# Who issues the stores of the normalised tiles: the load queue's engine or ScalarE

## The chip, the core and the metric

The kernel runs on one core of a Trainium2 chip. A core has five engines with instruction queues of their own: TensorE (PE, matrix products, with its weight loads shown as PEld), VectorE (DVE), ScalarE (ACT), GpSimd (POOL) and SyncE (SP). Here SP computes nothing: it only issues DMA transfers. Sixteen DMA engines do the moving. The metric is the device time of one execution in microseconds (us), the median of several runs.

## The reference

One inference step of a two-layer decoder on 1024 prompt positions and 8 decode positions, model width 2048, all in float32. Layer 0 is a pooling mixer, layer 1 a sliding-window attention; shared keys and values are projected between them.

```python
z = x @ w_in                       # 2048 -> 4096
u, gate = z[..., :2048], z[..., 2048:]
d = pool(u) - u                    # trailing windows 2/4/8/16 on four channel groups
y = (group_linear(d) * scale * silu(gate)) @ w_out
h = layer_norm(ALPHA * x + y)      # layer 0, the normalised tiles "h"
...
k, v = h @ w_kv                    # shared keys and values
q, gate = h @ w_in_b               # 2048 -> 4096
o = window_attention(q, k, v, sinks) * silu(gate)
y = layer_norm(ALPHA * h + o @ w_out_b)
```

Only the two `layer_norm` lines and the way in which their results leave the core are touched here.

## The kernel before

**Layout and phases.** Activations lie transposed: 128 channels on the partitions, positions along the free axis. The positions are cut into chunk 0 (512 positions) and chunk 1 (520: 512 prompt, 8 decode). The work runs as phases (`PHASES`, line 50): `ai` (input projection, pooling and gate of layer 0), `ao` (its output projection), `bi` (query and gate projections with attention), `bo` (output projection of layer 1), each for chunk 0 and chunk 1. The products are float32 made of rounded float32r parts: every weight tile and every activation tile is split into a high part (an ACT cast, line 506 or 839) and a low part (a DVE subtraction, line 521 or 848), and three matmuls per tile (lines 685 to 687, or 713 to 715) add high by high, high by low and low by high.

**Products.** Most phases use seven products in place of eight (Strassen's scheme): `seven` (line 597) runs products in the order 0, 2, 1, 5, 3, 4, 6 into three PSUM banks; each product is 24 matmuls. Between products small ACT and DVE instructions move bank contents: after product 0 ACT copies a bank negated into another (`p0`, line 624), after product 2 into SBUF (`p2`, line 630), after 1 (`p1`, line 633), after 5 (`p5`, line 639), after 3 (`p3`, line 645, with a DVE subtraction, line 646), after 6 (`p6`, line 658). They are written into the queues when the next product begins, so each has about one product's time before TensorE needs the bank again. Phase `bi` of chunk 0 begins with two plain parts (`unit`, line 699) of 24 wider matmuls per weight tile.

**The weight stream.** `begin` (line 533) keeps a stream of weight tiles of 512 KB going: loads (line 288, on SP) run up to seven tiles ahead of the products, casts four, low parts three. In the plain parts these are five, four and three. All buffers come from one pool of 54 slots in SBUF (`Mem`, line 140), so a load waits until the slot's last user is done.

**Layer norm.** `ln_gen` (line 985) is a generator that runs beside a later product phase, one step per product. It finishes the sums, makes the mean and the reciprocal deviation, then goes over eight tiles of 128 partitions by two by 512 (or 520) values: load the tile (line 998, SP), subtract the mean (line 1072, DVE; chunk 0 alone), multiply (line 1075, DVE), scale and shift by two ACT activations (line 1064), and store (line 1065). It is used three times: the tiles of `h` of chunk 0 during `ao` of chunk 1, of `h` of chunk 1 at the start of `bi` of chunk 0, and the output tiles `y0` of chunk 0 during `bo` of chunk 1, the last phase. `h` is read back later by line 829 (tiles for products) and line 1329 (residuals); of `h`, DVE also makes sums and differences of the same tiles in SBUF (lines 896 to 899), which POOL stores (line 900). The output of chunk 1 has code of its own at the end (`phase_end`, lines 1416 and on, with its stores at line 1503).

**Order.** The order of PE, DVE and ACT instructions is that of the source (`in_order`, line 86). The order on SP and POOL is set by the tile framework's scheduler. Each DMA counts up a counter when it has landed; the DMAs that SP and ACT issue take eight counters in turn (`DMAHW0` to `DMAHW7`), and a DMA is issued only when the one that used its counter before has landed.

Of the kernel before, what the change touches and what calls it, by code (L numbers as in the profile page):

```python
# [191 lines left out]
class Kern:  # L192
# [792 lines left out]
    def ln_gen(self, c, pre, acc, gc, bc, out, td):  # L985


        nc = self.nc
        T = CHUNKS[c][1]
        pre = dict(enumerate(pre))  # L990
        away = lambda p: self.act["p", c][:, 2 * p : 2 * p + 2, :]
        L = self.mem.full(2 * T)
        mu, rr = L.a[:, :T], L.a[:, T : 2 * T]

        def load(p):
            if p < 8 and p not in pre:
                pre[p] = self.mem.full(2 * T)
                nc.sync.dma_start(self.pair_view(pre[p], T), away(p))

        b2 = lambda x: x[:, None, :].to_broadcast([P, 2, T])  # L1000
        flat = lambda s: s.a[:, : 2 * T]
        a2 = self.pair_view(acc, T)
        load(0)
        mean, var = {}, {}
        put = lambda s, ps: nc.scalar.copy(mu[:, s], ps)
        if c == 0:
            s2 = self.pair_view(self.l_sq[0], T)
            steps = (
                self.j_steps(T, a2[:, 0], a2[:, 1], mean, acc), self.j_steps(T, s2[:, 0], s2[:, 1], var, self.l_sq[0])
            )  # L1010
            for k in range(3):
                for st in steps:
                    st[k]()
                yield
        else:
            yield
        yield from self.quiet()
        load(1)
        if c == 0:
            self.j_sum(T, mean, put)  # L1020
        else:
            self.j_sum32(T, [a2[:, 0], a2[:, 1]], put)
            acc.free()
        yield
        w = self.mem.full(2 * T)
        q, v = w.a[:, :T], w.a[:, T : 2 * T]
        if c == 0:
            nc.vector.tensor_mul(q, mu, mu)
        else:
            sq, sqs = self.mem.full(2 * T), {}  # L1030
            for p in range(10):
                load(p + 2)
                if p < 8:
                    t = self.pair_view(pre[p], T)
                    nc.vector.tensor_sub(t, t, b2(mu))
                if 1 <= p <= 8:
                    sqs[p - 1] = sq if p == 1 else self.mem.full(2 * T)
                    nc.scalar.activation(flat(sqs[p - 1]), flat(pre[p - 1]), AF.Square)
                yield
                if p > 2:  # L1040
                    nc.vector.tensor_add(flat(sq), flat(sq), flat(sqs[p - 2]))
                    sqs[p - 2].free()
                yield
            s2 = self.pair_view(sq, T)
            for go in self.j_steps(T, s2[:, 0], s2[:, 1], var, sq):
                go()
                yield
        yield from self.quiet()
        self.j_sum(
            T, var,  # L1050
            lambda s, ps: nc.vector.scalar_tensor_tensor(v[:, s], ps, EPS, q[:, s], op0=ALU.add, op1=ALU.subtract)
            if c == 0 else nc.vector.tensor_scalar(v[:, s], ps, EPS, None, op0=ALU.add),
        )
        yield
        self.rstd(v, rr, q)
        w.free()
        yield

        def affine(p):
            t = self.pair_view(pre[p], T)  # L1060
            for j in range(2):
                m = 2 * p + j
                g, b = (self.prm[:, i + m : i + m + 1] for i in (gc, bc))
                nc.scalar.activation(t[:, j], t[:, j], AF.Identity, bias=b, scale=g)
            nc.sync.dma_start(out[:, 2 * p : 2 * p + 2, :], t)

        for p in range(10):
            load(p + 2)
            if p < 8:
                t = self.pair_view(pre[p], T)  # L1070
                if c == 0:
                    nc.vector.tensor_sub(t, t, b2(mu))
                    if td is None:
                        yield
                nc.vector.tensor_mul(t, t, b2(rr))
            if 1 <= p <= 8:
                affine(p - 1)
                if td is None:
                    pre[p - 1].free(True)
            if td is not None:  # L1080
                yield
            if p >= 2 and td is not None:
                t = self.pair_view(pre[p - 2], T)
                self.t_ops(t[:, 0], t[:, 1], td, p - 2, T // 2)
                pre[p - 2].free(True)
            yield
        L.free()
# [1423 lines left out]
```

## Time and profile before

| | |
|---|---|
| three runs | 2311.78, 2307.44, 2310.27 us, median 2310.27 |
| the profiled execution | 2308.12 us, of which the span from first to last instruction is 2306.3 |
| mean granted TensorE clock over the span | 0.998 |
| DVE, ACT, POOL busy | 83%, 60%, 9% of the span |
| bytes moved by DMA | 654 MB, 284 GB/s on average |
| transfers issued by SP at line 1065 | 24 (16 of `h`, 8 of `out_y`) |

The profile is of one execution. A row of the timeline gives start, duration, engine, line, operation and tiles by name; equal neighbours are merged (`x2`), and their time then covers the wait between them. A row of the waits names who waited, who released it, the total in us, how often, and the longest. In the chain of waits each row is a piece of the path that ended last, with its start and length. `SPq` is SP's queue.

### The profile page before, as it was taken

To read this page: it belongs to the slowest core of one execution; us is meant where nothing else is said; L and a number is where in the kernel's file an instruction comes from. 1 tells how busy PE (TensorE), PEld (TensorE's weight loads), DVE (VectorE), ACT (ScalarE), POOL (GpSimd) and SP (SyncE) were. 2 spreads that over 40 slices of the span, in tenths; PEclk is the share of its full clock that TensorE was granted. 3 is DMA by queue.
4 is the path that set the end of the run, shared out by engine and by line. 5 is a ranking of instruction groups with operands and counts; after the bars stand their busy time and mean duration, and the time that the engine had idled before them with its cause. 6 is when DMAs were issued, how large, how long until landed. Compare 5 with 4: busy or idle time off the path is not lost.

```text
span 2306.3 us, 50594 instructions
## 1 busy us (share of the span) xinstructions
PE 2283.7 (99%) x20353; PEld 2213.7 (96%) x20353; DVE 1908.0 (83%) x2429; ACT 1387.0 (60%) x2551; POOL 218.8 (9%) x399
## 2 busy tenths in 40 slices
PE   9999999999999999999999999999999999999998
PEld 8999999999999999999879999999999999999998
DVE  8888889877878888998868888899876777878987
ACT  5544446544546546555566666785766768657655
POOL 0111110011010010000111111101100010000001
PEclk9999999999999999999999999999999999999999
DMA  7868679988889999999676666777787878799884
GB/s 259 282 248 308 234 254 325 320 301 295 304 310 313 344 352 374 328 381 364 210 265 235 229 238 231 276 273 265 254 269 230 272 266 295 242 325 335 285 304 149
DMA packets 256956, 654.07 MB, mean 284 GB/s; under 512 B 27824, under 2 KB 116944, under 8 KB 256720
## 3 DMA queue, kind: packets, MB, share of 16 engines
q1 hardware_dynamic: 213568, 496.49, 63.7%
q0 software_dynamic: 43152, 154.34, 17.4%
q8 instruction: 159, 2.61, 0.5%
q14 instruction: 77, 0.63, 0.1%
HBM read 473.50 MB, written 177.23 MB: 282 GB/s over the span
## 4 chain that ended last, share of the span: by engine, by line
PE 54%; DVE 2%; DMA 2%; ACT 1%; issue 1%; SPq 0%; POOL 0%; DVEq 0%; POOLq 0%; ACTq 0%
PE pD L685 14%; PE pD L687 14%; PE pD L686 14%; PE pO L1978 2%; PE pD L713 2%; PE pD L715 2%; PE pD L714 2%; PE pS L1900 2%; PE pS L1953 1%; DMA m<-swob 1%; PE pS L1978 0%; DVE m L521 0%; DMA m<-h 0%; DMA m<-in_wob 0%; DVE m L848 0%
## 5 line engine op out<-in xcount | busy, mean ns | idle before, releaser
L685 PE MATMUL pD<-m,m 128*128 128x260 f32 (+1 forms) x5088 | 1442.3, 283 | 8.2 <-ACT m L633 4.2
L687 PE MATMUL pD<-m,m 128*128 128x260 f32 (+1 forms) x5088 | 1434.9, 282 | 3.8 <-DVE m L521 3.6
L686 PE MATMUL pD<-m,m 128*128 128x260 f32 (+1 forms) x5088 | 1435.0, 282 | 0.0
L685 PEld LDWEIGHTS pD<-m,m 128*128 128x128 f32 x5088 | 959.5, 189 | 17.6 <-issue 7.2
L687 PEld LDWEIGHTS pD<-m,m 128*128 128x128 f32 x5088 | 960.2, 189 | 5.4 <-DVE m L521 5.4
L686 PEld LDWEIGHTS pD<-m,m 128*128 128x128 f32 x5088 | 959.6, 189 | 0.5
L521 DVE TENSOR_TENSOR m<-m,m 128x1024 fp32r<-128x1024 f32 x690 | 832.7, 1218 | 86.5 <-ACT m L506 36.4
L506 ACT CAST m<-m 128x1024 fp32r<-128x1024 f32 x690 | 720.1, 1049 | 238.4 <-DVE m L352 99.7
L352 DVE TENSOR_TENSOR m<-m,m 128x1024 f32<-128x1024 f32 x128 | 156.4, 1222 | 14.1 <-DMA m<-in_wia 6.3
L848 DVE TENSOR_TENSOR m<-m,m 128x1024 fp32r<-128x1024 f32 (+1 forms) x118 | 144.0, 1225 | 4.0 <-ACT m L839 3.1
L839 ACT CAST m<-m 128x1024 fp32r<-128x1024 f32 (+1 forms) x118 | 123.3, 1053 | 3.9 <-DMA m<-in_x 2.4
L646 DVE TENSOR_TENSOR m<-pD,m 128x260 f32<-128x260 f32 (+1 forms) x92 | 39.0, 424 | 101.4 <-ACT pD L645 93.7
L658 ACT COPY m<-pD 128x260 f32<-128x260 f32 (+1 forms) x88 | 32.8, 373 | 122.2 <-PE pD L687 121.6
L1936 ACT ACTIVATE m<-m,sm 128x128 f32<-128x128 f32 x256 | 99.3, 390 | 0.0
L1185 PE MATMUL pD<-m,m 128*128 128x260 f32 (+1 forms) x528 | 91.5, 323 | 0.0
L633 ACT COPY m<-pD 128x260 f32<-128x260 f32 (+1 forms) x92 | 34.4, 374 | 93.4 <-PE pD L687 93.4
L713 PE MATMUL pD<-m,m 128*128 128x512 f32 x224 | 89.1, 398 | 0.0
L715 PE MATMUL pD<-m,m 128*128 128x512 f32 x224 | 88.4, 394 | 0.0
L714 PE MATMUL pD<-m,m 128*128 128x512 f32 x224 | 88.1, 393 | 0.0
L630 ACT COPY m<-pD 128x260 f32<-128x260 f32 (+1 forms) x90 | 33.6, 373 | 89.3 <-PE pD L687 87.2
L1185 PEld LDWEIGHTS pD<-m,m 128*128 128x128 f32 x528 | 79.4, 188 | 8.2
L624 ACT ACTIVATE pD<-pD 128x260 f32<-128x260 f32 (+1 forms) x90 | 33.2, 369 | 83.5 <-PE pD L687 83.0
(258 smaller groups left out, 2143.3 us busy)
## 6 DMA issues: line engine op xcount, KB each, us to landing
m<-in_wib SPq DMA_DIRECT2D x132, 512.0 KB
m<-in_wia SPq DMA_DIRECT2D x128, 512.0 KB
m<-swoa SPq DMA_DIRECT2D x64, 512.0 KB
m<-swob SPq DMA_DIRECT2D x64, 512.0 KB
swia<-m POOLq DMA_DIRECT2D x56, 512.0 KB, 4.7
m<-swia SPq DMA_DIRECT2D x56, 512.0 KB
m<-in_woa SPq DMA_DIRECT2D x48, 512.0 KB
swib<-m POOLq DMA_DIRECT2D x48, 512.0 KB, 4.1
```

What stands on the lines that cost most here:

```text
L352: self.nc.vector.tensor_add(s[out].a[:, :1024], s[x].a[:, :1024], s[y].a[:, :1024])
L506: self.nc.scalar.copy(hi.r[:, :1024], self.stream[self.cast].src().a[:, :1024])
L521: self.nc.vector.tensor_sub(lo.r[:, :1024], s.src().a[:, :1024], hi.a[:, :1024])
L685: nc.tensor.matmul(ps[:, :TH], wh[:, s], h, start=new and k == 0, stop=False, skip_group_check=on)
L686: nc.tensor.matmul(ps[:, :TH], wh[:, s], l, start=False, stop=False, skip_group_check=on)
L687: nc.tensor.matmul(ps[:, :TH], wl[:, s], h, start=False, stop=k == 7, skip_group_check=on)
L713: nc.tensor.matmul(ps[:], wh[:, s], h, start=par == 0 and k == 0, stop=False)
L714: nc.tensor.matmul(ps[:], wh[:, s], l, start=False, stop=False)
L715: nc.tensor.matmul(ps[:], wl[:, s], h, start=False, stop=par == 1 and k == 7)
L839: self.nc.scalar.copy(h.r[:, :n], s.a[:, :n])
L848: self.nc.vector.tensor_sub(l.r[:, :n], s.a[:, :n], h.a[:, :n])
L1185: nc.tensor.matmul(ps[:, : cs.stop - cs.start], ws[:, s], d[:, cs], start=f0 and k == 0, stop=l0 and k == 3,)
```

## The change

One word of line 1065 changes: the engine on which the store of a normalised tile is issued.

```diff
-            nc.sync.dma_start(out[:, 2 * p : 2 * p + 2, :], t)
+            nc.scalar.dma_start(out[:, 2 * p : 2 * p + 2, :], t)
```

It holds for all 24 stores. No other line issues a DMA on ACT. PE, DVE and POOL keep their instructions in the same order.

On ACT, in the last phase (`bo` of chunk 1), this is the fifth store of `y0`; `L633` is the copy of `p1` (a PSUM bank `pD` to a slot `m`), `prm` holds scale and shift:

```order
 L506 CAST m_2989_27769<-m_2973_27648 128x1024
 L1064 ACTIVATE m_2950_27432<-m_2950_27432,prm 128x512 x2
+L1065 DMA out_y<-m_2950_27432 128x1024
 L633 COPY m_2928_27247<-pD_27723 128x260
 L506 CAST m_2992_27806<-m_2977_27688 128x1024
```

The store now stands between the activations that make the tile and the copy behind them; every store stands so, right behind its two activations.

On SP, in the same phase, these are the third and fourth store of `y0` among the loads of weights (`in_wob` and its sums `swob`) and of the residual (`h`):

```order
 L288 DMA m_2977_27688<-swob_150 128x1024
-L1065 DMA out_y<-m_2924_27209 128x1024
 L288 DMA m_2966_27582<-in_wob 128x1024
 L288 DMA m_2969_27614<-swob_149 128x1024
...
 L288 DMA m_2973_27648<-swob_149 128x1024
 L1329 DMA m_2976_27678<-h_95 128x1040
-L1065 DMA out_y<-m_2937_27324 128x1024
+L288 DMA m_2982_27727<-swob_150 128x1024
 L1329 DMA m_2980_27719<-h_95 128x1040
-L288 DMA m_2982_27727<-swob_150 128x1024
```

Both stores are gone from SP, and one weight load moves ahead of a residual load.

On ACT of the changed kernel, at the start of `bi` of chunk 0, the sixth and seventh store of `h` of chunk 1, with what each waits for:

```order
L1064 ACTIVATE m_1574_13307<-m_1574_13307,prm 128x520
L1065 DMA h_95<-m_1574_13307 128x1040 [waits DMAHW2_49,Activation_49]
L1064 ACTIVATE m_1579_13335<-m_1579_13335,prm 128x520 [waits DVE_49]
L1064 ACTIVATE m_1579_13335<-m_1579_13335,prm 128x520
L1065 DMA h_95<-m_1579_13335 128x1040 [waits DMAHW6_49,Activation_49]
L506 CAST m_1636_13870<-m_1624_13798 128x1024 [waits DMASW7_49]
```

Each store waits for ACT's own activation to be complete, and some, as here, for an earlier transfer that used the same counter; on SP of the changed kernel the user of `DMAHW2` before this store is the load of an `h` tile (line 829), and that of `DMAHW1` before the eighth store a small load of line 1756.

## The prediction

> **What bounds the kernel now.** I read the page's busy times first, then who TensorE waited for, over the whole span and in the three stretches in which the moved stores run.
>
> ```profile
> span 2306.3 us, 50594 instructions
> PE 2283.7 (99%) x20353; PEld 2213.7 (96%) x20353; DVE 1908.0 (83%) x2429; ACT 1387.0 (60%) x2551; POOL 218.8 (9%) x399
> PE pD L685 <- ACT m L633: 4.2, 1, 4.2
> PE pD L687 <- DVE m L521: 3.6, 7, 0.9
> PE pD L685 <- ACT pD L624: 2.2, 2, 1.3
> PE pD L685 <- ACT m L2163: 0.6, 1, 0.6
> ```
>
> TensorE is busy for 2283.7 of 2306.3 us; 22.6 us are all that anything but the products could give back. In the stretch from 940 to 1240 us, which holds the sixteen stores of `h`, the only wait of TensorE is the last row, 0.6 us; in that from 2150 to the end, with the eight stores of `y0`, it is the 4.2 us of the first row, and 1.3 us at the very end that the change doesn't reach. The moved stores and their makers:
>
> ```profile
> L1065 SPq DMA_DIRECT2D h<-m x16: 320/360/1335, 958.6 to 1165.9; - x16
> L1065 SPq DMA_DIRECT2D out_y<-m x8: 338/338/1252, 2172.4 to 2237.1; - x8
> L1064 ACT ACTIVATE m<-m,prm x48: 798/809/834, 957.0 to 2236.3; 128x512 f32<-128x512 f32 x32, 128x520 f32<-128x520 f32 x16
> ```
>
> (durations in ns: least, median, most). One store stands at the 4.2 us stall. The chain of waits there, and SP, ACT and the DMA engines before it (the last row is GB/s from 2180 to 2215 us in 40 slices of 0.875 us):
>
> ```profile
> 2196.68 10.03 DMA m<-h
> 2206.80 1.09 issue
> 2207.89 1.22 DVE m L1072
> 2209.11 1.15 DVE m L521
> 2210.28 1.04 ACT m L506
> 2211.32 1.42 ACT m L1064 x2
> 2212.74 0.27 ACT m L633
> 2213.06 0.58 PE pD L685
> ...
> SPq L288 <- DMA p<-m: 9.0, 1, 9.0
> 2193.26 0.38 SPq L1065 DMA_DIRECT2D out_y<-m  x1
> 2193.74 0.38 SPq L288 DMA_DIRECT2D m<-in_wob  x1
> 2194.21 1.30 SPq L288 DMA_DIRECT2D m<-swob  x1
> ...
> 2196.68 0.60 SPq L1329 DMA_DIRECT2D m<-h  x1
> 2197.39 1.25 SPq L1065 DMA_DIRECT2D out_y<-m  x1
> ...
> 2187.45 1.52 ACT L1064 ACTIVATE m<-m,prm 128x512 f32<-128x512 f32 x2
> 2195.38 1.52 ACT L1064 ACTIVATE m<-m,prm 128x512 f32<-128x512 f32 x2
> GB/s 215 318 356 309 234 225 136 215 262 351 419 411 190 62 0 61 257 220 379 384 257 183 314 370 356 370 337 436 416 418 422 399 431 404 426 407 412 421 403 417
> ```
>
> SP sat 9.0 us behind a slot whose tile was still being stored to `p`. Then it issued a burst, the moved third store first; the residual load (`m<-h`) went out at 2196.68 and took 10.03 us. DVE, in order, waited for it, and through the low part, the cast and two activations `p1`'s copy was late.
>
> The stall costs more than its 4.2 us, by the granted clock (third figure from the end):
>
> ```profile
> 2200.00:2209.00 9.00, 8.89 (x74) 1.00 1.02 394
> 2213.00:2214.00 1.00, 0.94 (x4) 0.50 1.00 410
> 2218.00:2219.00 1.00, 1.00 (x9) 0.85 0.78 266
> ```
>
> It is halved when TensorE comes back and full again at 2218.3 (0.85 means 0.3 us at half): 5.2 us at half speed, 2.6 us lost. So 6.8 us, 0.3% of the time, hang on this one stall.
>
> **The change part by part. SP.** 24 issues leave it: 24 × 0.36 = 8.6 us of SP's time. They shorten the kernel only where TensorE waits for a load, at this one stall: the third store's issue (2193.26 to the next at 2193.74, 0.48 us) no longer stands ahead of the residual load. SP's new order, one weight load ahead of a later residual, comes behind that load: nothing. At the start of `bi` loads move up a few places as well; TensorE waits for no load there: nothing.
>
> **The transfers.** The third tile is ready at 2187.45 + 1.52 = 2188.97, so its store now goes out while SP sits, and its 512 KB leave the burst: at the 420 GB/s of the row's end 1.25 us. Against that, the fourth store (ready at 2196.90) no longer queues behind the residual load (2197.39 after 2196.68) but runs beside it: up to 1.25 us back. And the third store now overlaps the end of the store to `p` on which SP waits, when the engines still moved 190 to 411 GB/s; at most its own 1.25 us later again, probably about 0.3. Bounds for the load's landing: 0.48 + 1.25 = 1.7 us earlier to 0.48 − 1.25 − 1.25, 2.0 us later. I take 0.2 earlier (0.48 less 0.3, the two bytes' shares cancelling).
>
> [...]
>
> **ACT.** It gains 24 issues, each behind a wait for its own activation. The trace has no DMA issue on ACT. From below: the overlap alone is lost (in the chain the copy starts at 2212.74, when the pair ends), so 0.1 us, and a gain is excluded, as nothing leaves ACT. The nearest row is SP's issue, 0.34 to 0.36 us; the longest store on SP took 1.34. I take 0.36 + 0.1 = 0.45 us.
>
> What is queued behind? Eight stores, four in each chunk-0 stretch, have a bank copy on which the next product but one rests (`p0`, `p1`, `p3`, or `p5` ahead of `p3`); the ninth is the fifth store of `y0`. Such a copy has the length of one product, less itself:
>
> ```profile
> 2189.80 0.28 PE L686 MATMUL pD<-m,m 128*128 128x260 f32 x1
> ...
> 2192.66 0.28 PE L686 MATMUL pD<-m,m 128*128 128x260 f32 x1
> ...
> ACT m L633 <- PE pD L687: 93.4, 70, 2.5
> ```
>
> The two are 24 matmuls apart, 2.86 us, one product. The last row shows that in 70 of these copies ACT stood ready and waited for TensorE (total us, times, longest). With 0.37 us for the copy and some 0.2 for the way to TensorE, 2.3 us are spare; the second store of `y0` has a little less, as its copy starts late. An issue of 0.45 us disappears in that; so would 1.34. At the fifth store nothing is spare: there the whole 0.45 us goes onto the stall.
>
> **The plain parts of `bi`.** Here two stores of `h` can hold ACT for long, since they also wait for another transfer's counter.
>
> ```profile
> 1149.05 3.76 SPq L1065 DMA_DIRECT2D h<-m  x3
> 1152.90 0.80 SPq L829 DMA_DIRECT2D m<-h  x1
> 1163.38 1.26 SPq L1756 DMA_DIRECT2D m<-rows  x2
> 1157.02 2.96 ACT L1064 ACTIVATE m<-m,prm 128x520 f32<-128x520 f32 x4
> 1162.47 1.52 ACT L1064 ACTIVATE m<-m,prm 128x520 f32<-128x520 f32 x2
> 1167.76 0.29 DVE L1762 TENSOR_TENSOR m<-m,m 128x128 f32<-128x128 f32 x1 [3.73 <-DMA m<-rows]
> ...
> 1149.82 0.40 PE L713 MATMUL pD<-m,m 128*128 128x512 f32 x1
> 1154.46 0.40 PE L715 MATMUL pD<-m,m 128*128 128x512 f32 x1
> ```
>
> The sixth store is ready at about 1158.5 (half of the 2.96 us) and needs the landing of the load issued at 1152.90; with the 10.03 us of the other `m<-h` that is 1162.9, a wait of 4.4 us. But three moved stores stood ahead of that load on SP; without them it may go out at 1149.05, and 0.6 us are left. The eighth is ready at 1163.99 and needs the load of line 1756, landed by 1167.76: 3.8 us. Together 4 to 8 us of ACT standing, with softmax work, casts and one bank copy behind. What covers it: the two PE rows are 20 matmuls apart, so a tile of 24 takes 5.6 us, and casts run four tiles, low parts three tiles ahead, 17 us. Cost nothing; with the cover gone, up to 8 us.
>
> **The sum**, against the profiled execution's 2308.12 us (span 2306.3 and 1.8 around it; 2.2 below the median of the runs): stall −0.2 (landing) + 0.45 (issue) = +0.25 us. The half-clock stretch began before TensorE came back, and 0.25 us more of waiting spends 0.25 us of it idle, which saves 0.12: +0.1 us in all. Everything else 0. On the median 2310.27 that is 2310.4 us, no change.
>
> **The rivals.** *The stall falls under the clock's limit.* Stalls of up to 1.3 us elsewhere (the waits' longest) left the clock full, this one of 4.2 did not. With the landing at its early bound (1.7) and the issue at its low one (0.1) the stall is 4.2 − 1.7 + 0.1 = 2.6 us. If the clock then stays, 4.2 + 2.6 − 2.6 = 4.2 us are won, 2306.1; if the stall goes altogether, 6.8, 2303.5. [...] Against it: the fourth store's bytes and the fifth's issue. 10%, half of them above the bound of 0.2% (4.6 us, about what a measurement of this kernel can tell from no change).
>
> *An issue on ACT is dear.* Past 2.3 us per store the spare time of the eight copies is gone: with cost c the loss is 8 × (c − 2.3) + c, 4.6 us at c = 2.6, and 8.6 at c = 3: 2319. For it: SP's own issues stretch when its queue is full (1.30 and 1.25 us above). Against: ACT's queue never holds more than a store or two. 6%.
>
> *ACT's standing in the plain parts comes through.* Were the 17 us of lead used up, by casts that can't be made up before the next loads land, up to 8 us: 2318. Against: ACT is 60% busy, and TensorE waits there for nothing but 0.6 us. 5%.
>
> *The change does nothing at all*, a store being no earlier on ACT than on SP: the same 2310, inside the forecast.
>
> **How the numbers follow.** The forecast, with the stall between 3.0 and 6.6 us (4.2 − 1.7 + 0.45 to 4.2 + 2.0 + 0.45; half of each step reaches the time, as above), holds 79%: 2309.7 to 2311.5, and with the runs' own spread (2307.44 to 2311.78) 2307 to 2313. Reaching to both sides' rivals, to one fully won clock and a first part of a dear issue, gives 2306 to 2314.5. Faster by over 0.2%: half of the first rival and a little for spread, 7%. Slower: the second and third, 11%. The same: 82%.
>
> **What would show it.** In the changed profile: ACT issues at line 1065 of 0.3 to 0.5 us; the wait of TensorE for `L633` near 2213 at 4 to 5 us, with the clock at half behind it; no new wait over 1 us between 940 and 1240; ACT standing at the sixth and eighth store of `h` of chunk 1 with nothing behind it late. Wrong if that stall is under 3 us or gone, if issues take over 2 us, or if TensorE waits for ACT in the plain parts.

## The result, and the profile after

| | before | changed |
|---|---|---|
| median of 13 runs each, beside each other on one chip | 2308.03 us | 2315.23 us |
| least and most | 2305.25 to 2311.78 | 2311.95 to 2322.44 |
| the profiled execution | 2308.12 us | 2312.09 us |

The changed kernel is slower: ratio 1.0034, 95% interval 1.0026 to 1.0042, and the medians differ by 7.2 us. The forecast was 2310.4 us and no change. The profiled execution of the changed kernel is the second shortest of its runs; that of a second profile, below, is the longest of its set.

The page of the changed kernel, and TensorE's waits (line waited for: total us, times, longest):

```profile
span 2310.3 us, 50584 instructions
PE 2283.6 (99%) x20353; PEld 2212.8 (96%) x20353; DVE 1907.7 (83%) x2429; ACT 1388.4 (60%) x2551; POOL 218.8 (9%) x399
PE pS L1900 <- DMA m<-rows: 6.6, 1, 6.6
PE pD L685 <- ACT m L633: 0.7, 1, 0.7
```

TensorE is as busy as before. The 4.2 us for `L633`, on which the prediction turned, are down to 0.7 here, and a wait that before did not have stands on top: line 1900, the score matmuls of the attention, waits 6.6 us for a transfer `m<-rows`. Those rows are the round trip by which the rotated part of a query tile is rearranged (the program calls it `rope`): SP writes 16 rows of the tile to DRAM and reads them back in another order (lines 1751 and 1756, `rows`), DVE rotates them (lines 1762 to 1764), POOL writes the outcome to DRAM (line 1766) and SP reads it back into the tile (line 1771). Eight transfers of 32 KB each, in four pairs that follow one another.

SP in the changed kernel around this round trip (start, us, issues; equal neighbours merged):

```profile
1150.55 0.38 SPq L829 DMA_DIRECT2D m<-th  x1
1151.03 0.88 SPq L829 DMA_DIRECT2D m<-h  x1
1152.01 3.11 SPq L829 DMA_DIRECT2D m<-th  x2
1157.24 3.71 SPq L1751 DMA_DIRECT2D rows<-m  x2
1173.03 1.26 SPq L1756 DMA_DIRECT2D m<-rows  x2
...
1182.55 0.79 SPq L1771 DMA_DIRECT2D m<-rows  x2
```

and the rows of before that go with it (its stores, line 1065, its load at 1152.90 and its line 1756 at 1163.38 stand in the prediction):

```profile
1148.57 0.38 SPq L829 DMA_DIRECT2D m<-th  x1
...
1155.51 1.39 SPq L1751 DMA_DIRECT2D rows<-m  x2
1156.99 1.46 SPq L829 DMA_DIRECT2D m<-th  x1
...
1174.23 0.83 SPq L1771 DMA_DIRECT2D m<-rows  x2
1178.48 1.26 PE L1900 MATMUL pS<-m,m 64*32 64x32 f32 x64
```

Line 1756 goes out as soon as line 1751 has landed, so the time between the two issues is what the first transfer took. Before, that was 7.9 us after its issue (1155.51 to 1163.38), now 15.8 us (1157.24 to 1173.03). What changed ahead of it is the order on SP. Between the load of 1148.57 and line 1751 before had three stores of `h` and one load, and the other two loads of line 829 came behind; now no store is there, and SP has sent four loads of 512 KB by then. The trace also records when each transfer lands. In both kernels line 1751 lands 0.2 us behind the last load of line 829 that stands ahead of it on SP: at 1163.32 after 1163.14 before, at 1172.96 after 1172.79 now. The end of the chain on TensorE, and its clock behind it (third figure from the end):

```profile
1186.92 1.49 PE L1900 MATMUL pS<-m,m 64*32 64x32 f32 x42 [6.64 <-DMA m<-rows]
1187.00:1193.00 6.00, 6.00 (x79) 4.82 (x80) 4.45 (x5) 2.52 (x4) 0.00 (x0) 0.73 0.76 272
```

Line 1771 goes out 8.3 us later than before (1182.55 against 1174.23). TensorE itself is 1.8 us later in this execution (free for line 1900 at 1186.92 − 6.64 = 1180.28, against 1178.48), so against TensorE the issue is 6.5 us late. Before, the transfer that releases line 1900, the first of the last pair, landed at 1175.96 and had 2.5 us to spare; here it also takes longer, 4.2 us in place of 1.7 (landed at 1186.79). 6.5 and 2.5 later, less the 2.5 spare, is the stall. When TensorE starts again its clock is at half: 0.73 over 6 us is 1.6 us lost, so 6.6 + 1.6 = 8.2 us for this one stall.

ACT at the moved stores, and the durations of the issues (ns: least, median, most):

```profile
L1065 ACTq DMA_DIRECT2D h<-m x16: 326/326/348, 959.4 to 1175.2; - x16
L1065 ACTq DMA_DIRECT2D out_y<-m x8: 338/338/2222, 2181.2 to 2241.1; - x8
1158.75 1.54 ACT L1064 ACTIVATE m<-m,prm 128x520 f32<-128x520 f32 x2
1163.43 0.33 ACTq L1065 DMA_DIRECT2D h<-m  x1
...
1168.35 1.52 ACT L1064 ACTIVATE m<-m,prm 128x520 f32<-128x520 f32 x2
1175.17 0.33 ACTq L1065 DMA_DIRECT2D h<-m  x1
```

An issue costs ACT 0.33 us in the median. One is dear, the first store of `y0`:

```profile
2181.23 2.22 ACTq L1065 DMA_DIRECT2D out_y<-m  x1
2183.90 0.39 PE L685 MATMUL pD<-m,m 128*128 128x260 f32 x1 [0.69 <-ACT pD L645]
```

TensorE waits 0.69 us for the bank copy behind it, which before it did not. At the sixth store ACT stands from 1160.29 to 1163.43 (3.1 us), at the eighth from 1169.87 to 1175.17 (5.3 us): 8.4 us together.

### The profile page after: what moved, and what is told of

Read it like the earlier page. It is cut to its first block, busy times and chain, and to the rows that moved or that the text cites. A ratio compares the mean times of both kernels' runs of the same rounds, so it can differ in the third digit from the quotient of the medians.

```text
span 2310.3 us, 50584 instructions
## 1 busy us (share of the span) xinstructions
PE 2283.6 (99%) x20353; PEld 2212.8 (96%) x20353; DVE 1907.7 (83%) x2429; ACT 1388.4 (60%) x2551; POOL 218.8 (9%) x399
## 5 line engine op out<-in xcount | busy, mean ns | idle before, releaser
L633 ACT COPY m<-pD 128x260 f32<-128x260 f32 (+1 forms) x92 | 34.4, 374 | 94.1 <-PE pD L687 94.1
```

## The experiments

**The theories.** *A, the order on SP:* with the stores gone from SP, loads that nobody needs yet get ahead of the rope's small first transfer, which then lands behind them. *B, the bandwidth:* the stores on ACT's own queue run beside the rope's transfers and take the DMA engines from them, wherever SP has put them. *C, ACT standing:* the 8.4 us at the sixth and eighth store make work late that TensorE needs. (C is the prediction's third rival.) Each run below was timed in five rounds beside before on the same chip; the differences are of medians there.

**The parts of the change.** Line 1065 with the stores of one use alone on ACT:

```diff
-            nc.scalar.dma_start(out[:, 2 * p : 2 * p + 2, :], t)
+            (nc.scalar if td is None else nc.sync).dma_start(...)   # y0 alone
+            (nc.scalar if c == 1 else nc.sync).dma_start(...)       # h of chunk 1 alone
+            (nc.scalar if c == 0 and td is not None else nc.sync).dma_start(...)  # h of chunk 0 alone
```

> Only the eight stores of y0 go to ScalarE; the sixteen of h stay on SP. Theory A (order on SP: in the plain part of bi, SP freed of the stores of h sends four loads of line 829 ahead of the rope transfer of line 1751, and the rope's tile reaches TensorE late): no wait at L1900, and the 4.2 us wait of TensorE for L633 near 2213 us falls under 1.5 us with its half-clock stretch, as in the profiled run of the changed kernel; 4.2 + 2.6 = 6.8 us less than before, 2301 to 2303. Theory C (ScalarE standing at the sixth and eighth store of h makes the loss): the same, as no store of h is touched. If the stall near 2213 had gone by chance in that one profiled run: 2308, as before. If an issue on ScalarE is what costs (24 x 0.3 us): 2310.

> Only the eight stores of h of chunk 1 (the plain part) go to ScalarE. Theories A (order on SP), B (the stores' ring shares the DMA engines with the rope's transfers) and C (ScalarE stands at the sixth and eighth store) all put the loss here: a wait of TensorE at L1900 of 5 to 8 us near 1187 us, half clock behind it for some 6.8 us, 6.6 + 1.6 = 8.2 us more than before, 2316; the wait of 4 us near 2213 stays. If the loss lies in the other stores or in the count of issues: under 2310.

> Only the eight stores of h of chunk 0 go to ScalarE. Theories A, B and C: no rope transfer that TensorE is near stands behind these, so the same as before within 2 us, 2306 to 2310, the wait near 2213 kept. If each issue on ScalarE costs its 0.33 us on the path: 2311.

| moved to ACT | median | before | ratio (95%) |
|---|---|---|---|
| the 8 stores of `y0` | 2307.27 | 2308.30 | 1.0001 (0.9992 to 1.0009) |
| the 8 of `h`, chunk 1 | 2317.08 | 2308.30 | 1.0032 (1.0019 to 1.0045) |
| the 8 of `h`, chunk 0 | 2309.21 | 2308.30 | 1.0005 (0.9996 to 1.0013) |

The whole loss lies in the eight stores of chunk 1, which fall into the plain part. That moving `y0` would win 6.8 us was a miss: nothing is won that can be measured. Who released TensorE by the profile with the stores of chunk 1 alone, ACT's eighth store, and the work that line 1900 needs:

```profile
PE pS L1900 <- ACT m L839: 4.4, 1, 4.4
1156.14 0.81 ACT L1917 COPY m<-pS 128x768 f32<-128x768 f32 x1
...
1166.67 1.52 ACT L1064 ACTIVATE m<-m,prm 128x520 f32<-128x520 f32 x2
1171.51 0.33 ACTq L1065 DMA_DIRECT2D h<-m  x1
1179.27 0.89 SPq L1771 DMA_DIRECT2D m<-rows  x2
1182.75 1.72 PE L1900 MATMUL pS<-m,m 64*32 64x32 f32 x48 [4.38 <-ACT m L839]
```

The profile names a cast of ACT's (line 839) as the releaser, but the name is inferred and wrong here. In the program, line 1900 waits for the two transfers of line 1771 and, of ACT, only for the copy of line 1917 that frees its bank. That copy had ended at 1156.95; the transfers, issued from 1179.27 on, landed at 1182.61, and line 1900 began at 1182.75. So the rope is late here too. But ACT had stood 3.3 us at the store, so A and C still had to be told apart.

**All stores on ACT, SP's loads held back.** The loads of line 829 in this phase are told to follow line 1751 on SP; they wait for nothing more. This holds back all five of them, more than the two that had got ahead, so it is not quite the order of before:

```diff
-        self.nc.sync.dma_start(t, src)                     # line 829
+        self.nc.sync.dma_start(t, src); behind(self)
...
+                nc.sync.dma_start(rows[j], ...); self.rope_at = ...  # line 1751, by name
...
+def behind(k):
+    if getattr(k, "ph", "") == "bi0" and getattr(k, "rope_at", None):
+        k.tc.add_manual_dep(   # order on SP alone
```

> All 24 stores on ScalarE as in the changed kernel, but the loads of line 829 in the plain part of bi chunk 0 may go out on SP only behind the rope's first transfer (line 1751); nothing else moves on any other engine. Theory A (order on SP): line 1751's transfer lands in about 8 us instead of 15.7, the wait at L1900 falls under 1 us, and with the stall near 2213 gone the kernel takes 2301 to 2303. Theory B (the stores on ScalarE's ring take the DMA engines from the rope's transfers): the wait at L1900 stays at 4 us or more, 2312 to 2316. Theory C (ScalarE stands): the same as B, since ScalarE still waits at the sixth and eighth store. A new wait for one of the held loads would be a cost of this edit: 3 us more.

TensorE's wait, and SP:

```profile
PE pS L1900 <- DMA m<-rows: 0.6, 1, 0.6
1156.18 1.09 SPq L1751 DMA_DIRECT2D rows<-m  x2
1157.37 1.47 SPq L829 DMA_DIRECT2D m<-h  x2
1160.23 1.53 SPq L1756 DMA_DIRECT2D m<-rows  x2
```

Line 1751 lands within 4.1 us, and the wait is 0.6. The median is 2309.53 against 2308.30, ratio 1.0000 (0.9991 to 1.0009): the loss is gone with all 24 stores still on ACT's queue. That is against B. It says little of C, because ACT stands less here as well, not at all at the sixth store and 0.9 us at the eighth; the expectation had it standing as before. The second half of the expectation, a gain from the stall near 2213, failed as with `y0` alone.

**Which stores of chunk 1.** Only pairs 2 to 4, which stood on SP between the loads; and only pairs 5 to 7, which hold those where ACT stands:

```diff
+            (nc.scalar if c == 1 and p in (2, 3, 4) else nc.sync).dma_start(...)
+            (nc.scalar if c == 1 and p in (5, 6, 7) else nc.sync).dma_start(...)
```

> Of the 24 stores only the third, fourth and fifth of h of chunk 1 go to ScalarE (pairs 2 to 4), those that stood on SP between the loads of line 829 in the plain part of bi; the sixth to eighth, at which ScalarE stands, stay on SP. Theory A (order on SP: two more loads of line 829 go out ahead of the rope's first transfer, line 1751): that transfer lands some 14 us after its issue, TensorE waits 4 to 7 us at L1900 near 1180 us, and the time is 5 to 8 us over before: 2313 to 2317. Theory C (ScalarE standing at the sixth and eighth store): no loss, 2307 to 2310, as ScalarE doesn't stand.

> Only the sixth to eighth store of h of chunk 1 go to ScalarE (pairs 5 to 7); the third to fifth stay on SP, whose order up to the rope's first transfer (line 1751) is that of before. Theory A (order on SP): line 1751 lands about 8 us after its issue as before, no wait over 1 us at L1900, 2307 to 2310. Theory C (ScalarE stands at the sixth and eighth store until other transfers have landed, and casts are late): ScalarE still stands 3 us or more at the eighth store, and TensorE loses 4 us or more: 2312 to 2316.

> Only the sixth to eighth store of h of chunk 1 on ScalarE once more: its first profiled execution was the longest of its runs (2317.09 us, with a wait of 3.2 us at L1900), while the median was 2310.18. Theory A: in an execution near the median the wait at L1900 is under 1.5 us, median 2308 to 2311. Theory C (ScalarE standing at these stores delays work): the wait at L1900 is 3 us or more in a median execution too.

The chain of waits with pairs 2 to 4 moved, and the clock behind it:

```profile
1155.67 12.42 DMA rows<-m
1168.15 2.13 DMA m<-rows
...
1183.00:1193.00 10.00, 10.00 (x91) 7.98 (x92) 5.85 (x7) 4.12 (x13) 0.00 (x0) 0.72 0.84 294
```

With three stores moved the rope's transfer takes 12.4 us, TensorE waits (4.2 us in the waits' row of `L1900`, released by `m<-rows`) and loses 2.8 more by the clock (0.28 of 10 us): 7.0. The median is 2315.01 against 2308.31, 6.7 us more, ratio 1.0028 (1.0017 to 1.0040), and ACT stands at none of the three: their issues follow their activations within 0.03 us. That refutes C as the cause of this loss.

With pairs 5 to 7 moved the median is 2310.18 against 2308.31 (1.0009, 1.0000 to 1.0018) the first time and 2307.66 against 2307.96 (1.0002, 0.9993 to 1.0010) the second. The second profile, TensorE's wait and ACT at the seventh store:

```profile
PE pS L1900 <- DMA m<-rows: 0.8, 1, 0.8
1160.07 1.53 ACT L1064 ACTIVATE m<-m,prm 128x520 f32<-128x520 f32 x2 [0.42 <-DVE m L1921]
1164.56 0.33 ACTq L1065 DMA_DIRECT2D h<-m  x1
```

ACT stands 3.0 us (1161.60 to 1164.56), and nothing is lost that both timings show. This profile is the longest of its runs (2311.59 us), and even there line 1900 waits 0.8. In the first profile (2317.09 us, the longest of that set too) it waited 3.2: with the stores running beside them the round trip's transfers can be late, but this is not what a usual run does. So ACT can stand some 3 us and no loss is seen. The longer standing of the changed kernel, 8.4 us in all, was not run without a late rope: at the eighth store ACT waits for the landing of line 1756, and that is late when the rope is.

**The rope's first transfer in another queue.** All stores on ACT, line 1751 of the plain parts issued by GpSimd:

```diff
-                nc.sync.dma_start(rows[j], ...)            # line 1751
+                (nc.sync if self.strassen else nc.gpsimd).dma_start(rows[j], ...)
```

> All 24 stores on ScalarE, and SP's loads of line 829 as early as in the changed kernel; but in the plain parts the rope's first transfer (line 1751) is issued by GpSimd, in a queue of its own. Theory A as a matter of queue position: this transfer no longer stands behind the loads and lands within 6 us though they are still in flight, so the wait at L1900 falls under 2 us, 2303 to 2310. Theory B (all transfers share the DMA engines' bandwidth, whatever the queue): it lands as late as in the changed kernel, 12 us or more after its issue, and the wait stays at 4 us or more: 2312 to 2316. GpSimd's other work behind the new issues could cost up to 2 us more in either.

```profile
PE pS L1900 <- DMA m<-rows: 1.2, 1, 1.2
1155.76 0.92 SPq L829 DMA_DIRECT2D m<-h  x1
1158.58 0.99 POOL L1751 DMA_DIRECT2D rows<-m  x2 [1.30 <-ACT m L2158]
1166.07 1.85 SPq L1756 DMA_DIRECT2D m<-rows  x2
```

Issued behind this and the other loads, but in another queue, it lands in 7.5 us (expected: within 6), half of the 15.8, and the wait is 1.2. It lands at 1166.06, ahead of the load of `h` that SP had issued before it at 1155.76 (1166.46). So the place in SP's queue is most of it. That it needs 7.5 and not the 4.1 of the run with the loads held may be a share for B, or may come from GpSimd's queue, where a store of 520 KB (line 900, landed at 1165.60) stood ahead of it. The median is 2311.77 against 2308.31, ratio 1.0015 (1.0006 to 1.0024), half of the loss and above the 2310 that was expected at most. 1.2 us of the 3.5 are the wait at line 1900; the rest I can't place. The edit is not quite clean: POOL's other stores moved, and SP's second load of `h` went out 4.7 us later than in the changed kernel (1155.76 against 1151.03).

**One load less ahead.** As the run with the loads held, but for one of the loads that had got ahead:

```diff
+    if getattr(k, "ph", "") == "bi0" and getattr(k, "rope_at", None) and k.since == 3:
```

> All 24 stores on ScalarE as in the changed kernel, but one of the two loads of line 829 that got ahead of the rope's first transfer (line 1751) in the plain part goes out behind it again. Theory A (order on SP): the loads ahead landed 4.7 us apart in the changed kernel (1163.35, 1168.62, 1172.79), so line 1751 lands some 4.7 us earlier and the wait at L1900 falls from 6.6 to about 2 us, the clock perhaps staying full: 4.7 to 6.3 us under the changed kernel, 2309 to 2311. Theory C (ScalarE stands) and theory B (bandwidth): the wait stays at 4 us or more, 2312 to 2316.

The chain, and the clock behind the wait (3.4 us at `L1900`):

```profile
1157.63 11.27 DMA rows<-m
...
1184.10:1193.00 8.90, 8.90 (x87) 7.07 (x88) 6.85 (x8) 5.18 (x10) 0.00 (x0) 0.70 0.63 204
```

The transfer takes 11.3 in place of 15.8 us, 4.5 less for one load, near the 4.7 that A expects. One profile each does not fix this figure, since behind the same four loads the transfer also took 14.0, 12.4 and 11.6 us in other profiles. But the wait fell by 3.2 only, to 3.4, and the median is 2314.37 against 2308.31, 6.1 us more, not the 1 to 3 I expected. The clock is most of it: this shorter stall is followed by 0.30 × 8.9 = 2.7 us lost, against 1.6 behind the longer one. 3.4 + 2.7 = 6.1.

**The changed kernel once more.** No edit.

> The changed kernel as it is, run and profiled once more beside the others. Its first profiled execution took 2312.09 us, near the least of its runs, with a wait of 6.6 us at L1900 and hardly any near 2213 us. Theory A: the wait at L1900 is there again with 4 us or more, median 2314 to 2316. If the wait near 2213 belongs to the kernel of before alone (y0's stores cure it): under 1.5 us again. If it comes and goes from run to run, as the runs of y0 alone suggest (same time as before): it can be anywhere from 0 to 5 us, and an execution over 2314 us has it.

The chain of waits in this execution (2319.70 us):

```profile
1152.11 7.68 DMA th<-m
...
1159.80 1.26 SPq L829
...
1161.15 11.63 DMA rows<-m
...
PE pS L1900 <- DMA m<-rows: 6.0, 1, 6.0
PE pD L685 <- ACT m L633: 3.4, 1, 3.4
```

The median is 2315.73 against 2307.96, ratio 1.0038 (1.0026 to 1.0051). The wait at line 1900 is there again, 6.0 us, and the chain names a second way in which the order hurts: one of the loads that got ahead reads `th`, a tile that POOL was still storing, so SP itself stood until 1159.80 and the rope's transfer behind it was issued only at 1161.15. The wait near 2213 is back with 3.4 us.

**The stall near 2213.** Before with the residual loads of the last phase (line 1329) issued by GpSimd, and the same together with the held loads and all stores on ACT:

```diff
-                nc.sync.dma_start(self.pair_view(xs[p], T), ...)   # line 1329
+                (nc.gpsimd if self.ph == 'bo1' else nc.sync).dma_start(...)
```

> The kernel of before (all stores on SP), with the residual loads of the output product of chunk 1 (line 1329, m<-h) issued by GpSimd in place of SP. If the stall near 2213 us hangs on SP's burst ahead of that load, as the prediction had it: the load goes out up to 6 us earlier, the wait of TensorE for L633 near 2213 is under 1.5 us and the clock stays full, 4.2 + 2.6 = 6.8 us less: 2301 to 2303. If the load is late by shared bandwidth or by its buffer: the wait stays, 2306 to 2310.

> All 24 stores on ScalarE, the loads of line 829 in the plain part of bi behind the rope's first transfer on SP (as in the run that held them), and the residual loads of the output product of chunk 1 on GpSimd. Theory A and the prediction's reading of the stall near 2213 together: neither wait is left, 2300 to 2303 in the median, 6 to 8 us under before. If only the first holds: 2307 to 2310, as with the held loads alone. If ScalarE's standing (theory C) or the shared engines (theory B) cost as well: 2304 to 2307.

The first of the two, TensorE's wait, POOL at the load in question and the chain:

```profile
PE pD L685 <- ACT m L633: 3.0, 1, 3.0
2196.85 0.55 POOL L1329 DMA_DIRECT2D m<-h  x1 [10.75 <-DVE m L521]
m<-h POOLq DMA_DIRECT2D x1, 520.0 KB, 8.3
2198.34 12.60 DMA m<-swob
...
2213.79 0.39 PE pD L685
```

Off SP the load goes out at 2196.85, against SP's 2196.68 before. TensorE is 1.9 us later here (it comes to the stall at 2213.79 − 2.96 = 2210.8, before at 2213.06 − 4.16 = 2208.9), so against TensorE the load goes out 1.7 us earlier, where up to 6 were expected. SP's burst had held it by about that much; for the rest it waits for the slot that it fills, on POOL 10.75 us. It lands in 8.3 us in place of 10.0, and then a weight load of 12.6 us ends a wait that is down to 3.0 us. The median is 2306.00 against 2307.96, ratio 0.9991 (0.9982 to 1.0000): perhaps 2 us won, at the edge of what can be told, where 5 to 7 were expected. The two together give 2308.99 against 2307.96, ratio 1.0003 (0.9995 to 1.0012); the 6 to 8 us that I expected are not there, with a wait of 2.2 us for `L633` left. No version clearly beats before.

## Why the prediction was wrong

**The step that failed** stands under SP: "At the start of `bi` loads move up a few places as well; TensorE waits for no load there: nothing." That TensorE waits for no load is true and is the wrong question. The loads move past line 1751, and TensorE depends on that. Before, line 1771 went out 4.25 us ahead of line 1900 (1174.23 to 1178.48): that is all that the round trip had to spare, its last transfer included (2.5 us once that had landed), and a wait list of before can't show it, since nobody waited. The order of the changed kernel, known without a run, has it in plain sight, five loads ahead of line 1751 where before had three and three stores:

```
L1771 DMA m_1605_13580<-rows_101 16x512 x2
L829 DMA m_1628_13821<-h_87 128x4x256
L829 DMA m_1633_13860<-th_84 128x4x256
L829 DMA m_1629_13823<-h_87 128x4x256
L829 DMA m_1632_13858<-th_84 128x4x256
L829 DMA m_1637_13889<-th_84 128x4x256
L1751 DMA rows_102<-m_1613_13667 16x512 x2
```

The loads that got ahead are the cause. With all five loads behind line 1751 the loss is 0 ± 2 us. With one of the two new ones behind it, it is 6.1. With the two brought forward by moving three stores alone it is 6.7, and with the order of before up to line 1751 and three later stores on ACT it is 0 to 2.

**Point by point.** *SP freed of 8.6 us:* right in size, 24 issues less; but with the stores gone loads run ahead, and that cost 7 us. In these runs the issuing engine decided the order as well, and the order left on SP, not the saved issues themselves, made the kernel 7.2 us longer.

*The stall near 2213 and the sum:* the estimate of +0.1 stands within its error (`y0` alone: ratio 1.0001, interval −1.8 to +2.1 us), but its reading was partly wrong. The burst on SP held the residual load by less than 2 us; before that it waited for its slot, as it does on GpSimd. And the stall is no constant. It was 4.2 us in the profile I read, 3.3 to 6.0 in the five others with the stores of `y0` and that load on SP, and from 0.4 to 4.1 in the six with the stores on ACT and the load on SP. The low end makes single profiles look like the first rival (2303.5 to 2306.1), and at this stall the first profile of the changed kernel did (0.7); the medians do not follow.

*ACT's issue:* 0.33 us measured in the median for 0.36. Sixteen of the stores, `y0` and `h` of chunk 0, show no loss in their two runs, so the rival that has every issue dear falls. But one of its signs was there: the first store of `y0` took 1.98 to 2.64 us in four of the profiles with all stores on ACT, and TensorE waited 0.45 to 1.10 us for the copy behind it. So that copy has about 1.5 us to spare (2.22 − 0.69), not the 2.3 worked out, and why this issue is long stays open. A full queue, the prediction's reason for SP's long issues, goes with SP's own record (in the trace of before, of SP's 154 issues with no whole transfer of its own in flight none took over 1 us, of the 1014 others 82 did) but not with this one: ACT had issued its store before at 1175.2, a thousand us earlier. (That rival's sum at c = 2.6 is 8 × 0.3 + 2.6 = 5.0 us, not 4.6.)

*ACT standing at two stores of `h`:* foreseen at 4 to 8 us and found at 8.4. No cost of its own was seen, as foreseen, though only some 3 us of it were run without a late rope. The third rival had the right place and size, up to 8 us in the plain part, but the wrong mechanism.

*The range* of 2306.0 to 2314.5 ended 0.7 us short of the median. The slower end was made from ACT's possible costs alone; no rival had a transfer on SP that gets later because others get earlier.

## What to carry to other kernels

An engine that only issues is also a schedule: taking transfers off its queue moves every later one up, and what was paced by them now runs ahead (here two loads of 512 KB, and 32 KB behind them took 15.8 us in place of 7.9). Look in the new order for small transfers of a dependent round trip, ask which large ones they now stand behind, and measure their spare time from the last issue to its reader, because a wait that is not there yet is in no list of waits. If the order gets worse, it can be put back by a rule on that one queue, without undoing the change. And a stall seen in one profile should be looked up in a second before a sum is built on it.

## What the runs showed of the hardware

**A short stall can cost as much as a long one.** Two stalls of about the same length, and TensorE's clock behind them (third figure from the end), first with `y0` alone moved, after 2.4 us near 2213, then with `h` of chunk 1 alone, after 2.2 us near 1962:

```profile
2213.00:2219.00 6.00, 6.00 (x51) 6.00 (x52) 6.00 (x7) 4.55 (x8) 0.00 (x0) 1.00 0.77 265
```

```profile
1962.40:1966.00 3.60, 3.60 (x18) 3.60 (x19) 1.78 (x2) 3.60 (x11) 0.00 (x0) 0.54 1.05 373
```

The first leaves it full, the second halves it for 3.3 us (0.46 × 2 × 3.6) and loses 1.7. In the profiles of before and of the changed kernel the clock is at half once between 7 us and the last product, for 6.83 us in both (2211.47 to 2218.30 and 1183.38 to 1190.21), and it falls 2.6 and 3.1 us after TensorE has stopped (2208.9 and 1180.28). The rows of the clock's record in each of these two traces begin whole multiples of 3.41 us apart: at 6.46 (the first), 2211.47, 2218.30 and 2303.63 before, which are 646, 2 and 25 of them, and at 5.79, 1183.38, 1190.21 and 2306.37 in the changed kernel, 345, 2 and 327. Why one of the two stalls above halves the clock and the other does not was not shown. Of the stalls of 3.4 to 6.6 us above, the longest lost least afterwards (1.6 us against 2.7 and 2.8): of its 6.8 us at half clock TensorE spent 3.5 idle (1183.38 to 1186.92). Were the other two stretches as long, their losses would leave 1.5 and 1.2 us of idle time (6.8 less twice the loss), an estimate as well. The prediction's first rival counted on a stall of 2.6 us to leave the clock full: that of 2.4 us did, that of 2.2 us did not.

**Place in a queue, and another queue.** The same 32 KB took 15.8, 14.0, 12.4 and 11.6 us in four profiles behind four loads of 512 KB in SP's queue, 11.3 with one load less, 7.9 behind two loads and three stores, 7.5 in GpSimd's queue beside the loads, and 4.1 with the loads held back.
